# Modulation rows, one sum product, a context norm and the final norm moved to other places in a two-layer backbone kernel

## The chip, the cores and the metric

The kernel runs on one core of a Trainium2 chip. The metric is the device time of one execution in microseconds (us). The engines are named PE (TensorE: PE for matmuls, PEld for weight loads), DVE (VectorE), ACT (ScalarE), POOL (GpSimd) and SP (SyncE, which issues most of the loads). Line numbers, as in L1263, are lines of the kernel before.

## What is computed

Two layers over 512 latent tokens `x` and 256 context tokens `ctx`, width 1024, all in float32. Each layer has an attention part and a SwiGLU feed-forward part (FFN, hidden width 2816). Ahead of each stands an RMSNorm with shift and scale, behind each a gated residual; shift, scale and gate come from a product of the conditioning vector with `ada_w`. In layer 1 the context is used for keys and values only. At the end stands an RMSNorm of the latent tokens.

```python
for layer in range(2):
    ctx_out = layer < 1
    mod_x = split((silu(c) @ ada_w[layer] + ada_b[layer]), 6)        # s = 0 .. 5; s = 5 is the FFN's gate
    mod_c = split(silu(c_ctx) @ ada_w[layer] + ada_b[layer], 6)
    h_x = rmsnorm(x, norm_g[layer, 0]) * (1 + mod_x[1]) + mod_x[0]   # h_c the same from ctx and mod_c
    o_x, o_c = mixer(h_x, h_c)                # layer 0: differential heads || 2-D neighbourhood heads
                                              # layer 1: windowed grouped-query attention with sinks
    x = x + mod_x[2] * o_x
    h_x = rmsnorm(x, norm_g[layer, 1]) * (1 + mod_x[4]) + mod_x[3]
    x = x + mod_x[5] * ((silu(h_x @ w1) * (h_x @ w3)) @ w2)
    if ctx_out:                               # the same three lines for ctx with mod_c
        ...
return rmsnorm(x, final_g)
```

## The kernel before

**Number format.** Activations lie transposed, features on partitions in eight tiles of 128. A float32 product is three matmuls: every operand is split into a high part (made on ACT) and a low part (the rest, made on DVE), and `mm3` adds high x high, low x high and high x low in one PSUM bank. `split` makes both parts with ACT and DVE; `split_by_dma` has the low part made by an accumulating DMA issued on POOL.

**Stages.** Layer 0's attention goes by eight pairs of heads (`u` = 0 to 7; from 4 on they are neighbourhood heads). A list of steps (four blocks of latent queries and one of the context, each with a first part `a`: scores and softmax, and a second part `b`: transposes and value product) is interleaved with fillers: the next pair's projections, modulation rows, and in the last pair the first half of the output projection (`prep`, `first_part`). Then come the FFN of layer 0, the attention of layer 1, and the FFN of layer 1.

**Weights.** A class `Stream` holds a list of weights in the order of use (`S.add`, `S.add_made`). `S.next()` hands out the next one, makes the parts of some items ahead and requests the loads of some more. Raw weights lie in three buffers (`raw` of `wpool`), parts in three (`wh`, `wl`). All weight loads are on SP's queue, in order.

**The order on an engine.** The program is written as one sequence, and a scheduler places its instructions on each engine by a simulated timeline, within the dependencies; so an engine's order can differ from the order of the text. `tc.issue_after(x)` keeps an instruction behind `x`. A tile taken from a pool waits until the readers of what lay in its buffer are done.

**Modulation rows.** For s = 2 to 4 of layer 0, and for s = 5 of layer 0 and all of layer 1, the product with `ada_w` is done on DVE: a row loads 512 KB (`raw`) and multiplies it with the two conditioning vectors, with the sums into `mod` (`ada_rows`, L269, L270). The first 24 rows (`row_pieces`) are fillers of pairs 4 to 6. The other 56 (`ada1`, the eight of s = 5 first) are done in layer 0's FFN by `rows(n, after)`, which keeps them behind a given instruction and requests the next load (`ada_request`, two buffers).

**FFN of layer 0.** Hidden tiles go by pairs `p` = 0 to 10. Pairs 0 and 1 are plain products (`plain_tile`). The others use a scheme of seven half-size products in place of eight (`seven`, for `w1` and for `w3`): it takes sums of weights (`pair_weights0`, L496 to L500) and of tokens. `token_sums` makes the token sums `t2`, `t3`, `t4`; `first_sum`, run after pair 1, makes `t1` in place of a part of `hb`. Their order in `seven` is (`b11`, `b21`), `t1`, (`t2`, `b22`), (`t3`, `t4`); the results are added up by L1263 to L1271, which also free the PSUM banks (`f`, eight of one buffer each). The down products (`down`) of a group run between the `w1` and the `w3` products of the next group's first pair; `to_residual` (L1275) adds them to `xr` and `cr` with the gate of s = 5.

**The end of that FFN.** `down_last` does the last group: first all token products, then the context products `m` = 0 to 7. After the context product `m` = 2 stands `next_norm`, the norm of the tokens for layer 1 (sums of squares in `sq_sum`; `rstd_of`, whose matmul with ones is L309; `h_make`, L350 to L352). After the last context product stands the context's norm, in slices of a `q` tile. `behind_g` splits the weights `w_c[8]` and `w_c[10]` behind the making of `g`; `w_c[11]` is split by the ordinary path (L158, L159). Layer 1's attention begins with `k_x(0)`, then `v_part` for the groups 1 and 2 (latent tokens) and 0 (context), then `k_c(0)`.

**The tail.** `down_last` of layer 1 goes by halves of the tokens. After its second half's third product stands `final_norm(0)`: squares and sums, the scaling by `final_g` on ACT (L1720), `rstd_of`, the products with the reciprocal root on DVE and POOL and the output DMAs (L1723, L1724). After the last product stands `final_norm(1)`. The norm's tiles share few buffers:

```python
        npool = PoolMap(
            ns_a0=(fp, "s", 2), ns_a1=(fp, "s", 2), ns_s=(fp, "q", 2), ns_h=(fp, "q", 2),
            ns_v=(fp, "s", 2), ns_y=(fp, "s", 2), ns_t=(fp, "s4", 1),
        )
```

Of the kernel before, what the change touches and what calls it, by code (L numbers as in the profile page):

```python
# [16 lines left out]
D = 1024  # L17
# [20 lines left out]
def tile_trunk(  # L38
# [265 lines left out]

    def rstd_of(ps, accs, dim, pool):
# [39 lines left out]
    def h_make(k, h, xk, r, l, i, v, pool):  # L345
# [6 lines left out]
        nc.vector.scalar_tensor_tensor(h[:, 1, :], t, b, f32(h[:, 0, :]), op0=ALU.add, op1=ALU.subtract)  # L352
# [132 lines left out]

    def pair_weights0(p):

        raws = []

        def fn(n, raw):  # L490
            add = nc.vector.tensor_add
            if n == 0:
                raws[:] = raw
# [15 lines left out]
        def add_w(w):  # L509
            for i in range(4):  # L510
# [18 lines left out]
    def behind_g(raw):  # L529
        hi, lo = S.part_tiles()  # L530
        with tc.issue_after(g_made[0].ins):
            nc.scalar.copy(hi, raw[0])
        with tc.issue_after(g_made[1].ins):
            nc.vector.tensor_sub(lo, raw[0], f32(hi))
# [5 lines left out]
    def weights0():  # L540
# [23 lines left out]
        for j in (8, 10):  # L564
            S.add_made([w_c[j]], behind_g)
        for j in (11, 9, 0, 1, 2, 3, 4, 5, 6, 7):
# [4 lines left out]


    ada1 = [(l, s_, k) for l, s_ in [(0, 5)] + [(1, z) for z in range(6)] for k in range(KT)]
    ada1_load, ada_raw = list(range(len(ada1))), []

    def ada_request(pool):
        if ada1_load:
            raw = pool.tile([P, 1024], F32, tag="ada", name="raw")
            nc.sync.dma_start(raw, ada_wT[ada1_load.pop(0)])
# [3 lines left out]
    with ExitStack() as st:  # L583
# [394 lines left out]
        rows = [(s_, k) for s_ in range(2, 5) for k in range(KT)]  # L978

        def row_pieces(n):  # L980
# [8 lines left out]
            for _ in range(n):  # L989
                s_, k = rows.pop(0)  # L990
                S.add(ada_wT0[s_ - 2, k], "ada")
# [23 lines left out]
        for u in range(8):  # L1015
# [14 lines left out]
            else:  # L1030
                for m in range(KT):
                    S.add(wo_ab[m])

# [45 lines left out]
                fl = [prep(0), prep(1), prep(2), prep(3)] + [first_part(t) for t in range(4)] + [prep(4), prep(5), prep(6)]  # L1079
# [37 lines left out]
    with ExitStack() as st:  # L1117
# [123 lines left out]
        def seven(c, u, first=lambda: None):  # L1241
# [19 lines left out]
            (g1,) = item("t1")  # L1261
# [3 lines left out]
            add(u, g2, u)  # L1265
            add(c[1], g1, u)
# [34 lines left out]
        def down_last(js):  # L1301
# [10 lines left out]
            for m in range(KT):  # L1312
# [547 lines left out]
```

## Time and profile before

| | before |
|---|---|
| median of 3 runs | 1652.71 us (1646.57 to 1653.13) |
| profiled execution, its own time | 1649.52 us |
| its span, first to last instruction | 1647.7 us |
| mean granted TensorE clock | 0.989 |
| busy: PE / PEld / DVE / ACT / POOL | 1567.5 / 1402.1 / 1251.1 / 749.2 / 272.6 us |
| rows L269 | 80 x 1.22 us |
| read from HBM | 160.45 MB |

A line of the timeline gives start, duration, engine, line, operation, output <- input with sizes and count, and in brackets the idle time of the engine just before it with what ended it. Ends of matmuls are modelled, and consecutive ones overlap. A "q" behind an engine's name stands for its queue of issued DMAs. In a line of stretches the busy times of PE, PEld, DVE, ACT and POOL are followed by the granted clock, the DMA engines' share and GB/s.

### The profile page before, as it was taken

To read this page: it belongs to the slowest core of one execution; us is meant where nothing else is said; L and a number is where in the kernel's file an instruction comes from. 1 tells how busy PE (TensorE), PEld (TensorE's weight loads), DVE (VectorE), ACT (ScalarE), POOL (GpSimd) and SP (SyncE) were. 2 spreads that over 40 slices of the span, in tenths; PEclk is the share of its full clock that TensorE was granted. 3 is DMA by queue.
4 is the path that set the end of the run, shared out by engine and by line. 5 is a ranking of instruction groups with operands and counts; after the bars stand their busy time and mean duration, and the time that the engine had idled before them with its cause. 6 is when DMAs were issued, how large, how long until landed. Compare 5 with 4: busy or idle time off the path is not lost.

```text
span 1647.7 us, 26339 instructions
## 1 busy us (share of the span) xinstructions
PE 1567.5 (95%) x10222; PEld 1402.1 (85%) x10222; DVE 1251.1 (76%) x2155; ACT 749.2 (45%) x1326; POOL 272.6 (17%) x313
## 2 busy tenths in 40 slices
PE   5999998999999899999999998999999999999996
PEld 3798887877888789999999996977788799989896
DVE  4758698976576888879798879587665987869685
ACT  4446554556244423333434254356655552525243
POOL 2222222345010000010100001254322000000001
PEclk9999999999999999999999999999999999999998
DMA  9323254644225556675766762411010432323321
GB/s 340 100 58 89 80 157 131 189 133 119 69 64 131 155 163 160 159 199 159 193 182 170 201 173 94 101 54 40 14 39 25 156 128 78 127 74 95 120 73 52
DMA packets 69508, 199.52 MB, mean 121 GB/s; under 512 B 6932, under 2 KB 19380, under 8 KB 69384
## 3 DMA queue, kind: packets, MB, share of 16 engines
q1 hardware_dynamic: 59464, 164.40, 32.1%
q0 software_dynamic: 9344, 32.92, 9.4%
q8 instruction: 81, 1.33, 0.3%
q10 hardware_dynamic: 576, 0.52, 0.1%
q14 instruction: 43, 0.35, 0.1%
HBM read 160.45 MB, written 4.86 MB: 100 GB/s over the span
## 4 chain that ended last, share of the span: by engine, by line
PE 58%; issue 7%; DMA 6%; DVE 6%; ACT 2%; POOL 0%; DVEq 0%; SPq 0%; POOLq 0%; ACTq 0%
PE f L1250 4%; PE f L1251 4%; PE f L1249 4%; PE f L1653 4%; PE f L1652 4%; PE f L1651 4%; PE f L1281 3%; PE f L1282 3%; PE f L1283 3%; DMA wl<-raw 2%; PE lin L207 2%; PE t L1485 2%; PE lin L208 2%; PE lin L209 2%; PE f L1705 2%
## 5 line engine op out<-in xcount | busy, mean ns | idle before, releaser
L196 ACT ACTIVATE wh<-raw 128x1024 fp32r<-128x1024 f32 (+1 forms) x94 | 90.2, 976 | 233.9 <-DVE raw L500 124.4
L207 PE MATMUL lin<-hb,wh 128*128 128x512 f32 (+1 forms) x456 | 161.3, 354 | 8.5 <-DVE q L369 2.2
L208 PE MATMUL lin<-hb,wh 128*128 128x512 f32 (+1 forms) x456 | 159.4, 349 | 0.1
L209 PE MATMUL lin<-hb,wl 128*128 128x512 f32 (+1 forms) x456 | 158.3, 347 | 0.0
L197 DVE TENSOR_TENSOR wl<-raw,wh 128x1024 fp32r<-128x1024 f32 (+1 forms) x94 | 104.7, 1119 | 34.7 <-ACT wh L196 32.6
L269 DVE SCALAR_TENSOR_TENSOR junk<-raw,tables 128x1024 bf16<-128x1024 f32 x80 | 97.6, 1220 | 20.1 <-DMA raw<-in_ada_wT_dram 19.8
L202 POOL DMA_DIRECT2D wl<-raw x41 | 35.7, 871 | 458.6 <-ACT wl L201 421.6
L1281 PE MATMUL f<-g,wh 128*128 128x512 f32 (+1 forms) x304 | 103.4, 342 | 6.0 <-DVE q L1263 5.0
L207 PEld LDWEIGHTS lin<-hb,wh 128*128 128x128 f32 x456 | 86.1, 189 | 22.8 <-issue 3.0
L159 DVE TENSOR_TENSOR wl<-raw,wh 128x1024 fp32r<-128x1024 f32 x62 | 81.4, 1313 | 29.8 <-ACT wh L158 27.0
L1282 PE MATMUL f<-g,wh 128*128 128x512 f32 (+1 forms) x304 | 103.4, 341 | 0.0
L1283 PE MATMUL f<-g,wl 128*128 128x256 f32 (+1 forms) x304 | 101.9, 338 | 1.2 <-DMA wl<-raw 1.2
L1652 PE MATMUL f<-hb,wh 128*128 128x256 f32 x360 | 101.7, 283 | 0.0
L1651 PE MATMUL f<-hb,wh 128*128 128x256 f32 x360 | 101.4, 283 | 0.0
L1653 PE MATMUL f<-hb,wl 128*128 128x256 f32 x360 | 101.2, 283 | 0.0
L158 ACT CAST wh<-raw 128x1024 fp32r<-128x1024 f32 x62 | 64.9, 1047 | 77.5 <-PE lin L208 23.6
L1250 PE MATMUL f<-hb,wh 128*128 128x384 f32 x288 | 96.3, 335 | 1.1 <-DVE hb L197 1.1
L1249 PE MATMUL f<-hb,wh 128*128 128x384 f32 x288 | 96.4, 335 | 0.7 <-ACT hb L196 0.7
L1251 PE MATMUL f<-hb,wl 128*128 128x384 f32 x288 | 96.3, 334 | 0.3 <-DMA wl<-raw 0.3
L208 PEld LDWEIGHTS lin<-hb,wh 128*128 128x128 f32 x456 | 86.3, 189 | 11.0 <-issue 0.9
L209 PEld LDWEIGHTS lin<-hb,wl 128*128 128x128 f32 x456 | 86.2, 189 | 10.3 <-issue 0.3
L336 POOL TENSOR_TENSOR ns_a<-ns_a,ns_s 128x256 f32<-128x256 f32 (+1 forms) x16 | 17.3, 1084 | 442.7 <-ACT ns_s L332 434.4
(397 smaller groups left out, 4953.7 us busy)
## 6 DMA issues: line engine op xcount, KB each, us to landing
raw<-in_w_dram SPq DMA_DIRECT2D x132, 512.0 KB, 3.8
raw<-in_ada_wT_dram SPq DMA_DIRECT2D x80, 512.0 KB, 4.2
wl<-raw POOLq DMA_DIRECT2D x41, 512.0 KB, 6.4
raw<-in_w_ab_dram SPq DMA_DIRECT2D x24, 512.0 KB, 4.4
raw<-in_ada_w_dram SPq DMA_DIRECT2D x16, 512.0 KB, 9.5
k<-k SPq DMA_DIRECT2D x16, 384.0 KB, 6.0
raw<-in_w_c_dram SPq DMA_DIRECT2D x12, 512.0 KB, 4.3
nb<-in_na_bias_dram POOLq DMA_DIRECT2D x16, 256.0 KB, 3.8
```

The source lines that it names most:

```text
L207: nc.tensor.matmul(ps, wh(k), xh(k), start=k == 0, stop=False)
L208: nc.tensor.matmul(ps, wh(k), xl(k), start=False, stop=False)
L209: end = nc.tensor.matmul(ps, wl(k), xh(k), start=False, stop=k == n - 1)
L1249: nc.tensor.matmul(ps, wh(k), b[:, 0, :], start=k == 0, stop=False)
L1250: nc.tensor.matmul(ps, wh(k), b[:, 1, :], start=False, stop=False)
L1251: nc.tensor.matmul(ps, wl(k), b[:, 0, :], start=False, stop=k == 3)
L1281: nc.tensor.matmul(ps, hi, g[:, 0, cols[v]], start=first, stop=False)
L1282: nc.tensor.matmul(ps, hi, g[:, 1, cols[v]], start=False, stop=False)
L1283: nc.tensor.matmul(ps, lo, g[:, 0, cols[v]], start=False, stop=last)
L1651: nc.tensor.matmul(ps, wh(k), b[:, 0, :], start=k == 0, stop=False)
L1652: nc.tensor.matmul(ps, wh(k), b[:, 1, :], start=False, stop=False)
L1653: nc.tensor.matmul(ps, wl(k), b[:, 0, :], start=False, stop=k == 3)
```

## The change

- The eight rows of layer 0's FFN gate (s = 5) become fillers of the last pair of heads: four ahead of the output weights in the stream, four between the first of these, in kind `ada` (their raw buffers are those of the weights). The FFN's own rows are 48, all of layer 1; none runs in pair 1 or after pair 2's `w1` products, two instead of one stand behind each piece of the first down product.
- For pair 2's `w1` the product with `t1` comes last (`late_sum`), its weight part is made last, and the results are added in another order.
- `next_norm` stands after the context product `m` = 4 instead of 2. The context's sums of squares stay at the end of the FFN; its reciprocal root and `h_make` go behind `k_x(0)` in layer 1's attention, into that stage's buffers.
- `w_c[11]` is split behind the fourth tile of the token norm (`h_made[3 - KT]`, the fifth from the end of the list).
- The second half's final norm gets accumulators and root in the buffers of `spool[0]`. The first half's output products and DMAs (`put_out(0)`) stand behind the last residual add.

```diff
 h_make:
-        nc.vector.scalar_tensor_tensor(h[:, 1, :], t, b, f32(h[:, 0, :]), op0=ALU.add, op1=ALU.subtract)
+        h_made.append((act, nc.vector.scalar_tensor_tensor(h[:, 1, :], t, b, f32(h[:, 0, :]), op0=ALU.add, op1=ALU.subtract)))
...
+    def late_sum(p, w):
+        return p == supers0[1][0] and w is w1
 pair_weights0:
-            if n == 1:
+            if n and not done:
                 add(spool0[0], a21, a22)
                 add(a21, a21, a11)
+                done.append(n)
...
-            for i in range(4):
+            for i in (0, 2, 3, 1) if late_sum(p, w) else range(4):
...
+        S.add_made([w_c[11]], lambda raw: behind(*h_made[3 - KT], raw[0]))
-        for j in (11, 9, 0, 1, 2, 3, 4, 5, 6, 7):
+        for j in (9, 0, 1, 2, 3, 4, 5, 6, 7):
             S.add(w_c[j])
...
-    ada1 = [(l, s_, k) for l, s_ in [(0, 5)] + [(1, z) for z in range(6)] for k in range(KT)]
+    ada1 = [(1, z, k) for z in range(6) for k in range(KT)]
...
-        rows = [(s_, k) for s_ in range(2, 5) for k in range(KT)]
+        rows = [(s_, k) for s_ in range(2, 6) for k in range(KT)]
...
+                rr = row_pieces(4)
                 for m in range(KT):
                     S.add(wo_ab[m])
+                    if m < 4:
+                        rr += row_pieces(1)
...
-                fl = [prep(0), prep(1), prep(2), prep(3)] + [first_part(t) for t in range(4)] + [prep(4), prep(5), prep(6)]
+                fl = [prep(m) for m in range(4)] + [first_part(t) for t in range(4)]
+                fl = [f for pair in zip(fl, rr) for f in pair] + [prep(4), prep(5), prep(6)]
...
 seven:
             p1, p2 = item("b11", "b21")
             nc.scalar.copy(u, p1)
-            (g1,) = item("t1")
+            if not late:
+                (g1,) = item("t1")
             g2, r3 = item("t2", "b22")
             add(c[0], p2, u)
             first()
             add(u, g2, u)
+            if late:
+                g3, r4 = item("t3", "t4")
+                nc.vector.scalar_tensor_tensor(c[3], g3, -1.0, u, op0=ALU.mult, op1=ALU.subtract)
+                add(c[2], r4, c[3])
+                (g1,) = item("t1")
+                add(c[1], g1, u)
+                nc.vector.tensor_sub(c[3], c[3], g1)
+                return add(c[1], r3, c[1])
...
 down_last of layer 0:
-                if m == 2:
+                if m == 4:
                     next_norm()
             q = q_tile()
-            pool = Carve([q[:, NC * i : NC * i + NC] for i in range(6)])
-            r = rstd_of(fps(), sq_sum(cr, pool), D, pool)
-            for k in range(KT):
-                h_make(k, hc[k], cr[k], r, 1, 0, 1, pool)
+            sums = [spool0[0][:, NC * i : NC * i + NC] for i in range(2)]
+            c_sums.extend(sq_sum(cr, Carve(sums + [q[:, NC * i : NC * i + NC] for i in range(2)])))
...
-                        end = plain_tile(2 * p + i, g)
-                        if p:
-                            rows(3, end)
-                        elif i:
+                        plain_tile(2 * p + i, g)
+                        if i and not p:
                             token_sums()
...
-                    rows(2 if p == 2 else 1, end)
+                    rows(1 if p > 2 else 0, end)
                     if late:
-                        down(hidden(supers0[n - 1]), (2,) if n > 2 else (1,))
+                        down(hidden(supers0[n - 1]), (1,) if n == 2 else (2,))
...
 attention of layer 1:
         k_x(0, w0)
+        r = rstd_of(linp(), c_sums, D, npool)
+        for k in range(KT):
+            h_make(k, hc[k], cr[k], r, 1, 0, 1, npool)
...
 FFN of layer 1:
+        def norm_tiles(i):
+            a = (spool[0], "sum", 2) if i else (fp, "s", 2)
+            return PoolMap(ns_a0=a, ns_a1=a, ns_s=(fp, "q", 2), ns_v=(fp, "s", 2), ns_y=a, ns_t=(fp, "s4", 1))
...
-            r = rstd_of(fps(), sq, D, npool)
+            gains.append((ts, rstd_of(fps(), sq, D, pool)))
+
+        def put_out(i):
+            ts, r = gains[i]
             for k in range(KT):
                 (nc.gpsimd if k in (1, 4, 7) else nc.vector).tensor_mul(ts[k], ts[k], r)
-                (nc.scalar if i and k % 2 else nc.sync).dma_start(out[:, k, c], ts[k])
+                (nc.scalar if i and k % 2 else nc.sync).dma_start(out[:, k, halves[i]], ts[k])
...
+            with tc.issue_after(end.ins):
+                put_out(0)
             final_norm(1)
+            put_out(1)
```

More of the change, by code (lines that the diff above doesn't have):

```diff
@@ L484, in tile_trunk @@
     supers0 = [[0, 1], [2], [3, 4], [5, 6], [7, 8], [9, 10]]
+    def late_sum(p, w):
+        return p == supers0[1][0] and w is w1
     def pair_weights0(p):
-        raws = []
+        raws, done = [], []
         def fn(n, raw):
@@ L492, in fn @@
             if n == 0:
-                raws[:] = raw
+                raws[:], done[:] = raw, []
             (a11, a12), (a21, a22) = ([half(z, i) for i in range(2)] for z in raws)
-            if n == 1:
+            if n and not done:
                 add(spool0[0], a21, a22)
                 add(a21, a21, a11)
+                done.append(n)
             if n == 2:
@@ L527, in tile_trunk, with behind @@
     g_made = []
-    def behind_g(raw):
+    def behind(act, dve, raw):
         hi, lo = S.part_tiles()
[L531 to L534, printed above, removed]
+        with tc.issue_after(act.ins):
+            nc.scalar.copy(hi, raw)
+        with tc.issue_after(dve.ins):
+            nc.vector.tensor_sub(lo, raw, f32(hi))
         return hi, lo
@@ L564, in weights0 @@
         for j in (8, 10):
-            S.add_made([w_c[j]], behind_g)
-        for j in (11, 9, 0, 1, 2, 3, 4, 5, 6, 7):
+            S.add_made([w_c[j]], lambda raw: behind(*g_made, raw[0]))
+        S.add_made([w_c[11]], lambda raw: behind(*h_made[3 - KT], raw[0]))
+        for j in (9, 0, 1, 2, 3, 4, 5, 6, 7):
             S.add(w_c[j])
     spool0, tpool, small_parts = [], [], []
-    ada1 = [(l, s_, k) for l, s_ in [(0, 5)] + [(1, z) for z in range(6)] for k in range(KT)]
+    c_sums = []
+    ada1 = [(1, z, k) for z in range(6) for k in range(KT)]
     ada1_load, ada_raw = list(range(len(ada1))), []
@@ L578, in ada_request @@
             raw = pool.tile([P, 1024], F32, tag="ada", name="raw")
-            nc.sync.dma_start(raw, ada_wT[ada1_load.pop(0)])
+            nc.sync.dma_start(raw, ada_wT[KT + ada1_load.pop(0)])
             ada_raw.append(raw)
@@ L990, in row_pieces @@
                 s_, k = rows.pop(0)
-                S.add(ada_wT0[s_ - 2, k], "ada")
+                S.add(ada_wT0[s_ - 2, k] if s_ < 5 else ada_wT[k], "ada")
                 out_.append(lambda s_=s_, k=k: f(s_, k))
@@ L1239, in plain_tile, with seven @@
             return split(gt[j][:, 0, :], gt[j][:, 1, :], z)
-        def seven(c, u, first=lambda: None):
+        def seven(c, u, first=lambda: None, late=False):
             def product(name, part):
@@ L1341, in tile_trunk @@
                     c = [q[:, H * i : H * i + H] for i in range(4)]
-                    end = seven(c, s_tile())
+                    end = seven(c, s_tile(), late=late_sum(p, w1))
                     act = nc.scalar.activation(q, q, AF.Silu)
@@ L1692, in to_residual @@
         def to_residual(m, ps, c):
-            nc.vector.scalar_tensor_tensor(x1[m][:, c], ps, mod[1][:, 5, 0, m : m + 1], x1[m][:, c], op0=ALU.mult, op1=ALU.add)
+            return nc.vector.scalar_tensor_tensor(x1[m][:, c], ps, mod[1][:, 5, 0, m : m + 1], x1[m][:, c], op0=ALU.mult, op1=ALU.add)
         def down(js):
@@ L1708, in down @@
                     to_residual(4 * i + m, ps[m], slice(0, NX))
-        fo = []
+        fo, gains = [], []
+        def norm_tiles(i):
+            a = (spool[0], "sum", 2) if i else (fp, "s", 2)
+            return PoolMap(ns_a0=a, ns_a1=a, ns_s=(fp, "q", 2), ns_v=(fp, "s", 2), ns_y=a, ns_t=(fp, "s4", 1))
         def final_norm(i):
             c = halves[i]
-            sq = sq_sum([x1[k][:, c] for k in range(KT)], npool, apart=i == 1)
+            pool = norm_tiles(i)
+            sq = sq_sum([x1[k][:, c] for k in range(KT)], pool, apart=i == 1)
             ts = []
@@ L1735, in down_last @@
                     )
-                    to_residual(m, ps, c)
+                    end = to_residual(m, ps, c)
                     if ci and m == 2:
                         final_norm(0)
+            with tc.issue_after(end.ins):
+                put_out(0)
             final_norm(1)
+            put_out(1)
         for n, sg in enumerate(supers):
```

1 line of the change is left out of this document (added).

## The prediction

> **What bounds the kernel now.** I read the first part of the page, then the waits of TensorE, then busy time by stretches, and only then the timeline around each wait.
>
> ```profile
> PE 1567.5 (95%) x10222; PEld 1402.1 (85%) x10222; DVE 1251.1 (76%) x2155; ACT 749.2 (45%) x1326; POOL 272.6 (17%) x313
> ```
>
> TensorE is busy for 1567.5 of 1647.7 us, and the change leaves its matmuls as they are in number and size. So the change can win only out of 80 us of TensorE idling, plus what TensorE loses at a lower clock. The waits say where that idling lies (waiter, releaser: total, times, longest):
>
> ```profile
> PE t L235 <- DMA raw<-in_ada_w_dram: 13.5, 3, 12.7
> PE f L309 <- DVE q L338: 5.5, 1, 5.5
> PE f L1281 <- DVE q L1263: 5.0, 1, 5.0
> PE f L309 <- DVE ns_a L338: 3.6, 1, 3.6
> PE f L309 <- DVE norm L338: 2.6, 1, 2.6
> ...
> PE f L1250 <- DVE hb L197: 1.1, 1, 1.1
> ...
> PE f L1249 <- ACT hb L196: 0.7, 1, 0.7
> ```
>
> The longest, the first weights' load, is not touched. The others are: two norms at the end of the first FFN (5.5, 2.6), its first down product (5.0), the first seven products' wait for the token sum `t1` (0.7 + 1.1), the final norm (3.6). The change reaches every one. What it adds goes where VectorE still has room (stretch, length; PE, PEld, DVE, ACT, POOL busy; clock; DMA):
>
> ```profile
> 285.00:335.00 50.00, 49.69 (x353) 43.74 (x352) 45.17 (x84) 23.57 (x54) 18.97 (x22) 1.00 0.57 181
> ...
> 340.00:385.00 45.00, 41.55 (x323) 32.72 (x322) 25.95 (x58) 25.90 (x70) 24.64 (x38) 1.00 0.47 134
> 385.00:440.00 55.00, 51.77 (x357) 42.39 (x355) 36.94 (x60) 27.24 (x57) 13.25 (x22) 1.00 0.32 96
> 553.00:580.00 27.00, 19.78 (x106) 17.95 (x105) 22.89 (x42) 10.92 (x17) 2.59 (x3) 0.92 0.77 215
> 580.00:612.00 32.00, 32.00 (x180) 28.21 (x179) 26.59 (x47) 7.83 (x8) 1.74 (x2) 0.96 0.53 140
> ```
>
> **1. The gate's eight rows leave the start of the FFN, and `t1` comes last.** One row is a 512 KB load and two VectorE products with their accumulator reads:
>
> ```profile
> L269 DVE SCALAR_TENSOR_TENSOR junk<-raw,tables 128x1024 bf16<-128x1024 f32 x80 | 97.6, 1220 | 20.1 <-DMA raw<-in_ada_wT_dram 19.8
> ...
> 572.10 0.08 DVE L270 DVE_READ_ACCUMULATOR junk<-raw,csr 128x1 f32 x1
> 572.10 1.02 DVE L197 TENSOR_TENSOR hb<-q,hb 128x384 fp32r<-128x384 f32 x2
> 577.07 1.22 DVE L269 SCALAR_TENSOR_TENSOR junk<-raw,tables 128x1024 bf16<-128x1024 f32 x1 [3.94 <-DMA raw<-in_ada_wT_dram]
> 578.22 0.55 DVE L1263 TENSOR_TENSOR q<-f,s 128x384 f32<-128x384 f32 x1
> ...
> 592.00 0.17 DVE L272 TENSOR_TENSOR mod<-mod,adab 128x16 f32<-128x16 f32 x1
> 592.21 4.29 DVE L1275 SCALAR_TENSOR_TENSOR res<-f,mod,res 128x512 f32<-128x512 f32 x8
> ```
>
> So a row costs VectorE 2 x 1.22 + 2 x 0.08 = 2.6 us, eight 20.8. Read the timeline as a chain: VectorE works through rows and `first_sum` until 573.1, then stands at the fifth row for 3.94 us because its load has not landed; behind it in order stands the add L1263, which frees a PSUM bank; TensorE waits for that bank. The residual adds (L1275) cannot run before 592.2, since the gate they multiply by is finished at 592.0 (L272). After the change no row runs between the plain pair and the first down product, the gate is there long before, and `t1`, made by `first_sum`, is wanted only behind `t2`, `b22`, `t3`, `t4`. The waits 5.0, 1.1 and 0.7 go: 6.8 us. The stall also cost clock:
>
> ```profile
> 578.83:590.21 11.38, 11.38 (x48) 9.50 (x49) 11.24 (x20) 3.25 (x4) 0.32 (x1) 0.85 0.30 102
> ...
> 1022.77:1031.53 8.76, 8.76 (x35) 7.21 (x35) 8.54 (x16) 4.78 (x9) 0.00 (x0) 0.81 0.08 32
> ```
>
> Behind it the granted clock is 0.85 over 11.38 us, 0.15 x 11.38 = 1.7 us. [...]
>
> What may be late next: the first down product now takes two rows a piece, so 580 to 612 holds about two rows more, 26.59 + 5.2 = 31.8 of 32 us on VectorE. It is full, but TensorE has the banks of one piece in hand; I charge 0.5. The changed order of weight parts (0, 2, 3, 1) makes both sums of weights ahead of the second item; these are the same adds, their input is free only once the accumulating DMA has read it, before as after, so nothing. Term: 6.8 + 1.7 - 0.5 = **+8.0** (ends: 3, if another bank wait takes over half of the 5.0 and its clock; 8.5).
>
> **2. What the rows cost in the last head pair.** 20.8 us of VectorE, eight 512 KB loads on SP's queue, in turn with the output weights in the same three raw buffers, and past the loads of earlier heads' outputs (`ar`) on that queue. Rows ran in the stretch from 285 on: there VectorE is 90% busy and TensorE idles 0.3 us. From 340 to 440 VectorE has 62.9 of 100 us, with the rows 83.7, still under those 90%. So most is hidden by matmuls. It is not free: TensorE already idles 3.4 + 3.2 us there, on chains through VectorE, ScalarE and GpSimd, and a row in front of a mask-and-maximum step delays it by up to 1.22 us. Ends: 0 (no work is taken away here, a gain is excluded) and 20.8 (no cover). Nearest is the 285 stretch; I take **-2.5**, about one and a half rows. If the cover fails, the weights are late next: a row holds the buffer in which the next of them lands. GpSimd is in these chains too, and rows slow it:
>
> ```profile
> 303.58 2.69 POOL L914 TENSOR_SCALAR p<-p,rs 128x512 f32<-128x512 f32 x2
> ...
> 322.63 3.69 POOL L950 TENSOR_SCALAR pc<-pc,rs 128x256 f32<-128x256 f32 x4 [8.46 <-DVE rs L766]
> ...
> 360.42 1.83 POOL L950 TENSOR_SCALAR pc<-pc,rs 128x256 f32<-128x256 f32 x4 [4.99 <-DVE rs L766]
> ...
> 377.32 1.35 POOL L914 TENSOR_SCALAR p<-p,rs 128x512 f32<-128x512 f32 x2
> ```
>
> The same scalings take 2.69 and 3.69 us in the stretch with rows, 1.35 and 1.83 in the one without. The last pair has four of the one and one of the other: 4 x 1.34 + 1.86 = 7.2 us at most, a rival below. [...]
>
> **3. End of the first FFN.**
>
> ```profile
> 996.10 0.75 DVE L1275 SCALAR_TENSOR_TENSOR res<-f,mod,res 128x512 f32<-128x512 f32 x1
> ...
> 1007.25 2.84 PE L309 MATMUL f<-norm,ones 128*128 128x512 f32 x6 [2.63 <-DVE norm L338]
> ...
> 1014.34 1.41 DVE L350 SCALAR_TENSOR_TENSOR norm<-res,amod,csr 128x512 f32<-128x512 f32 x2
> ...
> 1017.72 1.22 DVE L159 TENSOR_TENSOR wl<-raw,wh 128x1024 fp32r<-128x1024 f32 x1
> ...
> 1022.77 2.08 PE L309 MATMUL f<-q,ones 128*128 128x256 f32 x4 [5.50 <-DVE q L338]
> ...
> 1029.06 0.75 DVE L352 SCALAR_TENSOR_TENSOR hb<-norm,mod,hb 128x512 fp32r<-128x512 f32 x1
> ```
>
> With eight rows fewer in all, three left over ahead of the residual adds go (7.8 us of VectorE), and the adds no longer trail. The token norm's sum of squares is then ready early, and its matmul, two context products later in the order, finds no wait. But it still starts near 1007: what was waiting becomes context work. Then everything hangs on VectorE: first L350 7.1 us after that matmul, eight tiles made at 2 x 0.67 = 1.34 us each. Before, the last tile was done at 1029.7. After, the context's rescaling no longer stands between (three ops of 0.4 us), nor part of its sums and residual adds; the weight split L159 stays, only behind the fourth tile. I expect the last tile at about 1028, one more step of k's product, and the context's L309, now behind it, 1 us: 1.5 us sooner than the row 1022.77:1031.53 lets it be. So the waits 2.6 and 5.5 go but are mostly given back as short waits at VectorE's pace. The 24 context `h_make` instructions move into the attention stage, hidden by the two token v groups ahead of the first user. Term: **+1.5** (ends: -1 if that cover is short; 5.5 + 1.7 = 7.2 if the tiles keep pace).
>
> **4. The tail.**
>
> ```profile
> 1628.96 2.84 DVE L1723 TENSOR_TENSOR fo<-fo,ns_y 128x256 f32<-128x256 f32 x5
> ...
> 1631.72 0.47 DVE L1693 SCALAR_TENSOR_TENSOR res<-f,mod,res 128x256 f32<-128x256 f32 x1
> ...
> 1631.89 0.42 ACT L329 ACTIVATE ns_a<-res 128x256 f32<-128x256 f32 x1 [2.40 <-DVE fo L1723]
> ...
> 1634.28 2.08 PE L309 MATMUL f<-ns_a,ones 128*128 128x256 f32 x4 [3.55 <-DVE ns_a L338]
> ...
> 1636.15 1.06 PE L309 MATMUL f<-ns_s,ones 128*128 128x256 f32 x2
> ...
> 1637.25 0.47 ACT L313 ACTIVATE ns_t<-f,epst 128x256 f32<-128x256 f32 x1 [2.88 <-PE f L309]
> ...
> 1639.65 3.34 DVE L1723 TENSOR_TENSOR fo<-fo,ns_y 128x256 f32<-128x256 f32 x5
> ```
>
> Half 0's five output products stand ahead of half 1's residual adds, and half 1's accumulators wait for the buffer which those products read. With other buffers and the products behind the last add, squares run as residuals come. TensorE ends at 1634.28 - 3.55 = 1630.7; add 0.47, square 0.42, last matmul about 0.5: 1632.3 against 1637.2, 4.9 less. Half 0's products (2.84 us) and eight output DMAs on SP now run in the shadow of half 1's logarithm, exponential and square; VectorE may hold one step back for a product or two: 0.7. Term: **+4.2** (ends 1.5, if all of the 2.84 stands ahead of half 1's steps, and 4.9).
>
> **Sum.** 8.0 - 2.5 + 1.5 + 4.2 = 11.2 us. The profiled execution took 1649.5 (span 1647.7 and 1.8 around it), so 1638.3; the median 1652.7 is 3.2 above it, so 1641.5. I take **1641**.
>
> **Rivals.**
> - *GpSimd's stretch lies on the path.* 7.2 in place of 2.5: 1646. For it the four rows of GpSimd above; against it GpSimd's 24.64 of 45 us.
> - *The bank wait moves.* Part 1 gives 3: 1646. For it the 31.8 of 32 us on VectorE; against it TensorE's unbroken 32.00 of 32 in that stretch before.
> - *Half 0's outputs still stand ahead.* Part 4 gives 1.5: 1644.
> - *Slower: VectorE becomes the bound of the last head pair.* If rows interleave one to one with the steps and each stands ahead of what TensorE waits for, the parts give 13.7 - 20.8 = -7.1: 1660, and more if weights come late behind their buffers. It decides from 13.7 us exposed, two rows in three. Against it the 285 stretch.
>
> **How the numbers follow.** Forecast 0.50, GpSimd 0.17, bank wait 0.14, outputs 0.10, slower 0.09. About 0.5% (8 us) is what a measurement of this kernel tells from no change: under 1644 it is faster. That takes most of the forecast and some of the next three, 0.58; slower by over 0.5% needs more than full exposure of the rows, 0.07; the rest 0.35. Range 1632 (nothing charged for the rows, upper ends at the FFN's end) to 1652 (two of the middle rivals together).
>
> **What would show it.** Right: no wait of L1281 on L1263 and clock 1.00 at the FFN's start; the wait on `q` L338 gone, with several short waits on `hb` in its place; last L313 some 5 us nearer to the end of the down product; TensorE's idling from 340 to 440 up by 2 to 3 us. Wrong: that idling up by over 10 us, or a new wait over 3 us for a weight, a bank or the context's tiles.

## The result, and the profile after

The kernel after takes 1641.75 us in the median of 5 runs (1639.9 to 1643.57); the ratio to the kernel before is 0.9942, 95% interval 0.9927 to 0.9958. The forecast was 1641. The time came out as forecast, but largely by luck: two of the four terms are far off, step 2 (five times its price) and step 3 (four times its gain), and these two misses nearly cancel. Line numbers from here on are those of the kernel after, except in the experiments that start from the kernel before.

The first part of the page shows what the prediction read first: TensorE's matmuls are as before, 1571 us busy of a span of 1640.3.

```profile
span 1640.3 us, 26342 instructions
...
PE 1571.1 (96%) x10222; PEld 1405.2 (86%) x10222; DVE 1253.5 (76%) x2155; ACT 748.8 (46%) x1326; POOL 275.5 (17%) x313
```

TensorE's waits after (waiter, releaser: total, times, longest):

```profile
PE t L235 <- DMA raw<-in_ada_w_dram: 13.5, 3, 13.1
PE f L1305 <- DVE q L1290: 3.9, 1, 3.9
PE s L911 <- DMA k<-k: 3.8, 2, 2.0
PE t L981 <- DVE pt L974: 3.2, 2, 2.6
PE t L934 <- ACT at L948: 3.0, 2, 2.5
...
PE t L945 <- DVE pt L937: 2.0, 2, 1.8
```

The six waits of before that the prediction listed behind the first load are gone from the head of the list (the final norm's is 0.7 us now). In their place stand one new wait for a PSUM bank (L1305) and four kinds of wait in the first attention that have grown (L911 to L981; of L911's 3.8 us only the 2.0 are new, the rest lies ahead of pair 5 and was there before, with 1.7).

To place the difference I cut both profiled executions at the same events: the mask-and-maximum that opens head pair 5 (the ninth L914); the first matmul with ones of the FFN's latent norm (L312); the first matmul of pair 2's `w3` products; the first context product of the first FFN's `down_last`; the first matmul of `k_x(1)`; the last matmul of the last down product; the end of the last matmul with ones. The stretches between them, in us:

| stretch | before | after | difference | predicted |
|---|---|---|---|---|
| start to pair 5 (same code) | 317.31 | 315.13 | -2.18 | 0 |
| A: pairs 5 to 7, output projection | 156.04 | 167.75 | **+11.71** | +2.5 |
| B: FFN start, to pair 2's `w3` | 136.56 | 126.68 | **-9.88** | -8.0 |
| C: to `down_last`'s context part | 390.24 | 393.33 | +3.09 | 0 |
| D: end of the FFN, to `k_x(1)` | 50.81 | 44.33 | **-6.48** | -1.5 |
| E: second layer | 579.49 | 579.95 | +0.46 | 0 |
| F: tail, to the last norm matmul | 6.76 | 2.57 | **-4.19** | -4.2 |

They add up to -7.47, the spans differ by 7.4; the medians differ by 10.96 and the ratio makes it 9.6 us (7 to 12), so the profiled pair lies at the low end. A stretch also differs between executions of the same code: C is 388.5 to 392.3 us in the four kernels below that have before's code there (before, e1, e2, e10), and the start to pair 5 is 315.1 to 318.8 in all.

The stretches of the prediction's windows, in the order it had them (length; PE, PEld, DVE, ACT, POOL busy; clock; DMA):

```profile
340.00:385.00 45.00, 36.94 (x253) 28.37 (x253) 40.90 (x78) 21.80 (x54) 26.61 (x32) 0.92 0.66 196
385.00:440.00 55.00, 50.57 (x354) 40.28 (x353) 33.55 (x61) 30.67 (x70) 15.70 (x27) 0.97 0.37 105
553.00:580.00 27.00, 27.00 (x158) 25.52 (x157) 23.23 (x43) 14.90 (x22) 2.59 (x3) 1.00 0.50 112
580.00:612.00 32.00, 32.00 (x185) 28.36 (x185) 25.40 (x44) 8.31 (x9) 1.74 (x2) 1.00 0.63 168
```

The FFN's start is what was forecast: no idling, clock 1.00. The attention is not. From 340 to 440 TensorE idles 8.06 + 4.43 = 12.5 us, against 3.45 + 3.23 = 6.7 before, and the clock, 1.00 before, is 0.92 and 0.97: 0.08 x 45 + 0.03 x 55 = 5.3 us more. Idling 5.8 and clock 5.3 make 11.1 of the 11.7 us of stretch A.

### The profile page after: what moved, and what is told of

Same layout as the page of the kernel before. It is cut to its first block, busy times and chain, and to the rows that moved or that the text cites. A ratio compares the mean times of both kernels' runs of the same rounds, so it can differ in the third digit from the quotient of the medians.

```text
span 1640.3 us, 26342 instructions
## 1 busy us (share of the span) xinstructions
PE 1571.1 (96%) x10222; PEld 1405.2 (86%) x10222; DVE 1253.5 (76%) x2155; ACT 748.8 (46%) x1326; POOL 275.5 (17%) x313
## 4 chain that ended last, share of the span: by engine, by line
PE 79%; DVE 10%; DMA 5%; issue 3%; ACT 1%; POOL 0%; SPq 0%; DVEq 0%; ACTq 0%; POOLq 0%
PE f L1264 5%; PE f L1266 5%; PE f L1265 5%; PE f L1676 4%; PE f L1675 4%; PE f L1674 4%; PE lin L207 3%; PE lin L208 3%; PE f L1305 3%; PE f L1306 3%; PE f L1307 3%; PE lin L209 3%; PE f L207 3%; PE f L208 3%; PE f L209 3%
## 5 line engine op out<-in xcount | busy, mean ns | idle before, releaser
L269 DVE SCALAR_TENSOR_TENSOR junk<-raw,tables 128x1024 bf16<-128x1024 f32 x80 | 99.3, 1241 | 13.7 <-DMA raw<-in_ada_wT_dram 13.2
L1305 PE MATMUL f<-g,wh 128*128 128x256 f32 (+1 forms) x304 | 103.8, 343 | 3.9 <-DVE q L1290 3.9
L1306 PE MATMUL f<-g,wh 128*128 128x256 f32 (+1 forms) x304 | 103.4, 341 | 0.0
```

The lines of the kernel that those rows point to most:

```text
L1305: nc.tensor.matmul(ps, hi, g[:, 0, cols[v]], start=first, stop=False)
L1306: nc.tensor.matmul(ps, hi, g[:, 1, cols[v]], start=False, stop=False)
```

## The experiments

Each kernel was timed in five rounds against the kernel before; the table gives the ratio and the stretches of its profiled execution.

| kernel | median us | ratio (95% interval) | A | B | C | D | F |
|---|---|---|---|---|---|---|---|
| before | 1652.71 | 1 | 156.0 | 136.6 | 390.2 | 50.8 | 6.8 |
| after | 1641.75 | 0.9942 (0.9927 to 0.9958) | 167.8 | 126.7 | 393.3 | 44.3 | 2.6 |
| e1 tail only | 1647.18 | 0.9971 (0.9958 to 0.9984) | 156.1 | 138.0 | 392.0 | 51.1 | 2.6 |
| e2 FFN end only | 1643.53 | 0.9952 (0.9935 to 0.9970) | 155.7 | 136.9 | 388.5 | 45.0 | 6.8 |
| e3 gate rows out | 1630.02 | 0.9864 (0.9844 to 0.9884) | 154.9 | 126.7 | 391.2 | 43.8 | 2.6 |
| e4 rows late | 1637.20 | 0.9918 (0.9898 to 0.9937) | 162.4 | 126.7 | 391.1 | 44.4 | 2.6 |
| e5 rows and `t1` only | 1648.42 | 0.9978 (0.9960 to 0.9996) | 170.5 | 126.7 | 391.0 | 47.9 | 6.8 |
| e6 `t1` in order | 1642.41 | 0.9942 (0.9920 to 0.9965) | 166.2 | 126.7 | 394.6 | 43.8 | 2.6 |
| e7 rows held in pair 7 | 1642.43 | 0.9943 (0.9922 to 0.9964) | 166.7 | 126.7 | 394.2 | 44.4 | 2.6 |
| e8 rows spread | 1635.71 | 0.9908 (0.9886 to 0.9929) | 160.1 | 126.7 | 393.9 | 44.1 | 2.6 |
| e9 `v` held | 1649.33 | 0.9993 (0.9980 to 1.0006) | 165.5 | 126.7 | 393.8 | 49.4 | 2.6 |
| e10 FFN end, norm at `m` = 2 | 1647.27 | 0.9973 (0.9958 to 0.9989) | 156.0 | 137.6 | 392.3 | 47.6 | 6.0 |
| e11 spread, sums on GpSimd | 1633.99 | 0.9897 (0.9881 to 0.9913) | 160.7 | 126.7 | 391.5 | 44.3 | 2.6 |
| e12 rows short | 1638.47 | 0.9926 (0.9908 to 0.9944) | 164.1 | 126.7 | 392.9 | 44.1 | 2.6 |

Two theories went in. T1, from the table of stretches: the rows cost about 11 us in the attention, the FFN's start pays 10, its end 6.5, the tail 4. T2, the prediction's terms: 2.5, 8.0, 1.5, 4.2.

**e1: the tail alone.** The kernel before with the new final norm:

```diff
+        def norm_tiles(i):
+            a = (spool[0], "sum", 2) if i else (fp, "s", 2)
...
+            with tc.issue_after(end.ins):
+                put_out(0)
             final_norm(1)
+            put_out(1)
```

> The kernel before with the final norm's part alone (norm_tiles, put_out, the returned residual update). Both theories sum the whole 11 us gain from parts, and this part at 4.1 to 4.2 us: about 4 us under the kernel before (0.9975 of its time; 1648.5 if it stands at 1652.7), nothing moved ahead of 1627 us, the last L309 matmul of the norm some 7 us nearer the end of the down product. Rival: the final norm is worth less alone, because half 0's multiplications and outputs were hidden anyway: 1.5 us.

Measured: 0.9971, 4.8 us, and stretch F goes from 6.76 to 2.57, in this kernel as in after. The tail is a part by itself, worth what was forecast.

**e2: the end of the FFN alone.** The kernel before with `next_norm` after `m` = 4, the context's sums kept, the rest of its norm behind `k_x(0)` and `w_c[11]` split behind a tile of the token norm:

```diff
-                if m == 2:
+                if m == 4:
                     next_norm()
...
         k_x(0, w0)
+        r = rstd_of(linp(), c_sums, D, npool)
+        for k in range(KT):
+            h_make(k, hc[k], cr[k], r, 1, 0, 1, npool)
```

> The kernel before with the end of the first FFN alone changed (x norm after the fifth context product, context's sums at the end of the FFN, the rest of its norm behind k_x(0), w_c[11] behind a context tile). Theory T1, from the milestones of the two traces: the start of k_x(1) comes 6.5 us nearer the start of the last down product, so 6.5 us under the kernel before (0.996). Theory T2, the prediction's step: 1.5 us under it (0.999), the waits given back at VectorE's pace; the 6.5 us of the trace would then hang on something that the other parts do.

Measured: 0.9952, and stretch D falls by 5.8, without any other part. That is T1; the step's 1.5 is wrong.

**e10: the same, with the norm again after `m` = 2.**

```diff
-                if m == 4:
+                if m == 2:
```

> The kernel before with the new end of the first FFN, but the x norm started after the third context product as in before, not after the fifth. It parts the 6.4 us of the kernel with the whole new end. Theory T1: the move to the fifth product is worth the 2.63 us wait on the x norm's sums that the third has, so about 4 us under before (0.9975), with a wait of about 2.6 us on L311 that comes back near 1007 us. Rival: the norm started earlier ends earlier, its h tiles are ready when the down product ends, and this kernel is as fast as the whole new end or faster (0.995 or less), since the 1.5 us wait on hb at the start of k_x(0) goes.

Measured: 0.9973, stretch D 47.6, and the wait of 2.88 us on the norm's sums stands there again, at 1010 us. So D's gain of 5.8 is 3.3 for the context norm behind `k_x(0)` (with the split of `w_c[11]`) and 2.5 for the two products.

**e9: the `v` products held behind `k_x(0)`.** On after:

```diff
-            v_group(ps, g, w)
+            with tc.issue_after(k_end.ins):
+                v_group(ps, g, w)
...
-        k_x(0, w0)
+        k_end = k_x(0, w0)
```

> The kernel after with the v products (L399 to L401) held until the first k product over the x tokens (k_x(0)) has ended, so that they can't stand between its matmuls. Theory T1: these products are what PE does while VectorE makes the eight h tiles (1018.6 to 1030.7 us in after, 12.1 us, of which k_x(0) alone fills 6). Without them PE idles 5 to 6 us more between 1018 and 1031, in short waits on hb, as the prediction had it, and the time is 5 to 7 us over after (1646.5 to 1648.5). Theory T2 (the v products fill nothing that matters, the gain is the removed wait on q and the context's norm behind k_x(0) alone): as after, within 1.5 us.

Measured: 0.9993, 7.6 us over after, a little beyond T1's range; in the profile stretch D is 49.4, 5.1 more than after and 1.4 less than before (the profiled execution is the fastest of this kernel, 1646.64 us, so the stretches don't hold the whole 7.6). The 1.4 is close to the prediction's +1.5. The timeline of this kernel shows the short waits that it described:

```profile
1017.83 0.50 PE L208 MATMUL t<-hb,wh 128*128 128x512 f32 x1 [0.46 <-DVE hb L355]
...
1025.06 0.50 PE L208 MATMUL t<-hb,wh 128*128 128x512 f32 x1 [1.66 <-DVE hb L355]
...
1026.72 0.50 PE L208 MATMUL t<-hb,wh 128*128 128x512 f32 x1 [0.70 <-DVE hb L355]
...
1028.38 0.50 PE L208 MATMUL t<-hb,wh 128*128 128x512 f32 x1 [0.70 <-DVE hb L355]
```

In after, at the same place, the `v` products (L399 to L401) stand between the `k` matmuls and need the same tiles:

```profile
1018.62 0.50 PE L207 MATMUL t<-hb,wh 128*128 128x512 f32 x1 [1.49 <-ACT hb L354]
1018.95 0.40 PE L399 MATMUL t<-wh,hb 128*128 128x256 f32 x2
1019.58 0.80 PE L208 MATMUL t<-hb,wh 128*128 128x512 f32 x1 [0.23 <-DVE hb L355]
1020.18 0.63 PE L209 MATMUL t<-hb,wl 128*128 128x512 f32 x1
1020.60 0.63 PE L207 MATMUL t<-hb,wh 128*128 128x512 f32 x1
1021.03 0.41 PE L400 MATMUL t<-wh,hb 128*128 128x256 f32 x1
...
1023.57 0.81 PE L312 MATMUL lin<-res,ones 128*128 128x256 f32 x3
```

Each tile that VectorE finishes feeds both the three matmuls of `k_x(0)` and those of the two latent `v` groups, so TensorE keeps step (busy for 11.00 of 11 us from 1020 to 1031), and the context's L312 comes without a wait.

**e5: the rows and `t1` alone.** After with the old end of the FFN and the old tail (`next_norm` at 2, the context's norm at the end, the final norm as before).

> The kernel before with the moved gate rows and the last t1 alone (old end of the first FFN, old final norm). Theory T1 (attention loses 9 to 11.5 us to the rows, the FFN start gains 10, the down product of pair 3 gives back 1 to 3): no gain that can be told, 0.998 to 1.001 of the kernel before. Theory T2, the prediction's steps 1 and 2 (gain 8.0, cost 2.5): 5.5 us faster, 0.9967.

Measured: 0.9978. The interval holds the prediction's 0.9967 and about half of T1's range, so the time doesn't tell them apart. The stretches do: A is 14.5 us longer than before, B 9.8 shorter. D is 2.9 shorter with the old code there: fewer rows are left ahead of the residual adds, and the wait of 2.63 us goes by that alone, as the prediction said.

**e6: `t1` third again.** On after:

```diff
     def late_sum(p, w):
-        return p == supers0[1][0] and w is w1
+        return False
```

> The kernel after with t1 again third in the first seven products of pair 2 (the rows stay where after has them). If t1's place carries a part of the gain at the FFN start, one of the waits of before returns there (0.48 to 1.09 us each, 565 to 574 us in before, or 4.97 us at the first down product), and this kernel is 1 to 5 us slower than after (1643 to 1647 beside 1641.75). If the rows alone filled VectorE there, it stands within 1 us of after and the waits stay away.

Measured: 0.9942, as after; B is 126.68 in both, and TensorE has no wait from 553 to 612 us. Once the rows are out of the FFN's start, the place of `t1` is worth nothing that shows.

**e3: the eight rows left out.** On after, neither loaded nor multiplied (the gate is zero):

```diff
+    nc.gpsimd.memset(mod[0][:, 5], 0.0)
...
-                ada_rows(0, s_, k, [tables, rbuf], S.next(), junk)
+                if s_ < 5:
+                    ada_rows(0, s_, k, [tables, rbuf], S.next(), junk)
...
-                S.add(ada_wT0[s_ - 2, k] if s_ < 5 else ada_wT[k], "ada")
+                if s_ < 5:
+                    S.add(ada_wT0[s_ - 2, k], "ada")
```

> The kernel after with the eight gate rows left out of the last head pair altogether (neither loaded nor multiplied; the FFN's gate is set to zero, so the output lacks the first FFN's contribution); everything else as in after. Theory T1: the eight rows cost the attention 9.5 to 11.5 us, since they run in the steps of pair 6 in which VectorE has no idle time: 9.5 to 11.5 us under the kernel after (1630 to 1632 beside 1641.75). Theory T2, the prediction's step: they cost 2.5 us: 1639. Were the loss in attention from another thing in the change (the order of the weight loads around pair 7, a run's difference), this kernel would stand where after stands.

Measured: 0.9864, 0.78% or 12.9 us under after, and A is 154.9 (12.8 us under after). The rows, loads included, are the price, and it is five times the term.

**e7: the rows kept in pair 7.** In after the scheduler had put them earlier than the text has them: row instructions of the gate start at 337.05, beside the steps of pair 6. Here each is held until its own step:

```diff
+                        step_mx[0] = nc.vector.tensor_tensor_reduce(
...
+                if s_ == 5:
+                    with tc.issue_after(step_mx[0].ins):
+                        ada_rows(0, s_, k, [tables, rbuf], raw, junk)
```

> The kernel after with each gate row held until the attention step of the last head pair in which the program text puts it (behind that step's row maximum), so that the eight rows run in pair 7 and not in pair 6, where after ran them. This is the place that the prediction priced at 2.5 us. If that price was right and only the place was wrong: 7 to 9 us under after (1633 to 1635), no new waits at 340 to 380 us. If VectorE bounds the last head pair (the prediction's slower rival): as after or slower, with the 13 us of idling moved to 380 to 435 us. Between: 1636 to 1640, the rows cost about 5 us there.

Measured: 0.9943, as after; A is 166.7. The rows are where the prediction had them, and cost as much. Its stretches show the price moved from the first to the second, with VectorE 95% busy:

```profile
340.00:385.00 45.00, 41.06 (x303) 32.12 (x301) 21.91 (x50) 22.95 (x64) 23.55 (x39) 0.97 0.35 96
385.00:440.00 55.00, 45.95 (x316) 35.76 (x315) 52.30 (x89) 29.78 (x60) 18.80 (x20) 0.99 0.52 174
```

So the size was wrong, not the place: this is the prediction's slower rival in part. In the five kernels with the rows in the last two pairs stretch A is 9.5 to 14.5 us longer than before, not 20.8.

**e12: the rows loaded, but multiplied over 8 of 1024 columns** (the gate is wrong by that):

```diff
+                n = D if s_ < 5 else 8
+                ada_rows(0, s_, k, [z[:, 0:n] for z in (tables, rbuf)], S.next()[:, 0:n], junk[:, 0:n])
```

> The kernel after with the eight gate rows loaded as in after (8 x 512 KB on SP's queue) and multiplied over their first 8 of 1024 columns alone, so that each of the 16 row instructions takes VectorE a tenth of its time (the FFN's gate is wrong by that). It parts the rows' loads from their 22 us on VectorE; the kernel without the rows left both out and was 11 us under after. Theory V: VectorE's time is the whole price, so this kernel stands where that one did, within 2 us (0.9864 to 0.988 of before). Theory L: the loads pay a part, since they stand on SP's queue ahead of the transfer of k halves and of weights (the wait on k<-k was 2.02 us in after and 0.91 in before): 3 us or more of the 11 remain (0.989 or more).

Measured: 0.9926, only 0.16% (2.6 us) under after, with overlapping intervals; A is 164.1, 3.6 under after and 9.2 over e3. That is Theory L: VectorE's time is not the whole price. With most of it gone (0.17 us a product in place of 1.22), VectorE reaches the rows before their loads have landed and stands there:

```profile
DVE pt L937 <- PE t L934: 6.9, 3, 2.8
DVE junk L269 <- DMA raw<-in_ada_wT_dram: 6.5, 4, 2.1
```

and ScalarE waits 4.2 us once for an output weight whose load stands behind the rows' on SP's queue; the DMA engines are 69% busy from 340 to 385 us (66% in after, 48% in e3). In after no row waits for its load from 320 to 440 us. One wait of TensorE can be followed back to the loads: the copy L974 stands behind two rows that wait, and TensorE behind the copy.

```profile
341.17 0.17 DVE L269 SCALAR_TENSOR_TENSOR junk<-raw,tables 128x8 bf16<-128x8 f32 x1 [2.14 <-DMA raw<-in_ada_wT_dram]
...
343.03 0.17 DVE L269 SCALAR_TENSOR_TENSOR junk<-raw,tables 128x8 bf16<-128x8 f32 x1 [1.48 <-DMA raw<-in_ada_wT_dram]
...
343.13 0.69 DVE L974 COPY pt<-t 128x512 f32<-128x512 f32 x1
...
343.87 1.08 PE L981 MATMUL t<-pt,v 128*64 128x256 f32 x6 [2.05 <-DVE pt L974]
```

So the loads and the rows' places in VectorE's order, with little of VectorE's time, are enough for 9.2 of the 12.8 us of stretch A. Whether VectorE's time alone would cost as much isn't shown: no kernel had the rows' time without their loads, none had the loads without the rows, and none had the loads at another place in the queue alone.

**e4: the rows one behind each product of the output projection's second half.** On after:

```diff
-                rr = row_pieces(4)
+                rr = []
                 for m in range(KT):
                     S.add(wo_ab[m])
-                    if m < 4:
-                        rr += row_pieces(1)
+                    if m > 3:
+                        rr += row_pieces(2)
...
-            w = S.next(0 if t >= 2 else 2)
+            w = S.next(2)
...
                 wo_chunk(m, w, "x", 4)
+                rr.pop(0)()
```

So the loads of the rows move with them, and the parts of two items are made ahead in all of that half.

> The kernel after with the eight gate rows taken out of the last head pair and put one behind each product of the second half of the output projection (430 to 475 us, PE without idle time, VectorE about half busy). Theory T1: the 9.5 to 11.5 us come back but for a little: 1631 to 1634, faster than both kernels. Theory T2: 1639 to 1641. Rival: the 8 x 3.3 us on VectorE there hold up the residual updates and so the projection's banks and the FFN norm: then a new wait on L1076 or L1083 or a later norm matmul, and no gain.

Measured: 0.9918; A is 162.4, 5.3 under after, about half of what T1 hoped. Two rows still ran at 371 and 377 us, beside the steps of attention. TensorE now waits for residual updates that stand behind rows, 4.3 us in five waits from 400 to 480:

```profile
PE lin L207 <- DVE res L1076: 3.2, 3, 1.6
PE lin L207 <- DVE res L1083: 1.1, 2, 0.6
```

A product of that half takes TensorE 12 x 0.23 = 2.8 us, a row and an update 2.6 + 0.75 = 3.35 on VectorE: a single product doesn't cover a row.

**e8: half as dense.** Four rows behind every second product, four behind the held context products, each held until the context product before it:

```diff
                     if m > 3:
                         rr += row_pieces(1)
+                rr += row_pieces(4)
...
-            w = S.next(0 if t >= 2 else 2)
+            w = S.next(2)
...
+                    with tc.issue_after(before[0].ins):
+                        ada_rows(0, s_, k, [tables, rbuf], raw, junk)
...
+                if m % 2:
+                    rr.pop(0)()
```

> The kernel after with four of the eight gate rows behind every second product of the second half of the output projection and four behind its held context products, each held until the context product before it. The run with one row behind each product won 4 us and paid 4.4 us of bank waits (L1076 and L1083) and 1.8 us for two rows that ran at 370 to 383 us. Theory T1: with half as many rows a product the bank waits fall under 1.5 us and the two early rows are gone: 1632 to 1634, 8 to 10 us under after. If the residual updates wait for the rows all the same: 1637, as the run with one a product.

Measured: 0.9908, 1635.71; A is 160.1, 7.7 under after. The time lies just above the expected 1632 to 1634. One row still ran early, at 368 us, in spite of the hold, and the waits for residual updates (L1082, L1089) are 2.0 us in place of 4.3. The wait for a PSUM bank in the FFN is 4.1 us here (L1315 on L1300), as in after.

**e11: e8 with two sums of weights on GpSimd.**

```diff
-                add(spool0[0], a21, a22)
-                add(a21, a21, a11)
+                eng = nc.gpsimd if p == supers0[2][0] and first_w[0] else nc.vector
+                first_w[0] = False
+                eng.tensor_add(spool0[0], a21, a22)
+                eng.tensor_add(a21, a21, a11)
```

> The kernel with the gate rows spread over the output projection, and in it the two sums of weight blocks of pair 3's first seven products (L502 and L503 in after, 128x512) on GpSimd in place of VectorE. In after VectorE waited 7.04 us in L502 for a weight's load, with the addition that frees PSUM (L1290) behind it, and PE waited 3.94 us for that; the spread kernel had 4.13 us there. Theory: it is the order on VectorE; with the sum elsewhere the wait falls under 1.5 us and the kernel is 2 to 4 us under the spread one (1632 to 1634). Rival: the load itself is late, and PE waits the same time a product later for the weight t1: 1635 to 1637.

First the wait that it aims at, in after's timeline:

```profile
637.21 0.55 DVE L1281 TENSOR_TENSOR s<-f,s 128x384 f32<-128x384 f32 x1
644.81 0.69 DVE L502 TENSOR_TENSOR res<-raw 128x512 f32<-128x512 f32 x1 [7.04 <-DMA raw<-in_w_dram]
645.42 0.55 DVE L1290 TENSOR_TENSOR q<-f,s 128x384 f32<-128x384 f32 x1
...
646.02 0.58 PE L1305 MATMUL f<-g,wh 128*128 128x256 f32 x1 [3.94 <-DVE q L1290]
```

VectorE stands 7 us at the sum L502 for a weight's load, and behind it in order stand the additions that free the banks. Measured: 0.9897, 1633.99. My edit missed: it moved the sums of pair 3's `w1`, which run at 607 us, and the blocking one belongs to its `w3`. The order on VectorE changed all the same, as this kernel shows:

```profile
632.62 0.56 DVE L1304 SCALAR_TENSOR_TENSOR q<-f,q 128x384 f32<-128x384 f32 x1
...
640.70 0.69 DVE L504 TENSOR_TENSOR res<-raw 128x512 f32<-128x512 f32 x1 [5.00 <-DMA raw<-in_w_dram]
...
643.95 0.64 PE L1317 MATMUL f<-g,wh 128*128 128x512 f32 x1 [2.32 <-DVE res L1311]
```

Now all additions stand ahead of the sum, the sum still waits, and TensorE loses 2.3 us in place of 4.1, for a residual add. Stretch C is 2.3 shorter than e8's. So the place of that sum among the additions matters; that GpSimd helped is not shown. By time e11 and e8 can't be told apart; e11 and after can (0.9913 against 0.9927 where their intervals are nearest). By median it is the fastest version that computes everything.

## Why the prediction was right, point by point

- **The total** was right largely by luck. Against the forecast stand +9.2 us (step 2) and +3.1 (stretch C), and on the other side -1.9 (step 1's own stretch), -5.0 (step 3), and 2.2 by which the profiled run was ahead at 315 us. With 0.5 in the second layer that leaves 3.7 us in this profiled pair: 7.5 were gained, not 11.2. By the ratio it is 9.6, by the medians 10.96; the median of before from which the forecast was counted, 1652.7, lies 1.3 to 1.9 above the four that were taken with the experiments (1650.8 to 1651.4).
- **Step 1** (predicted 8.0): stretch B gave 9.9, somewhat more than the 6.8 of waits and 1.7 of clock. Its charge of 0.5 for what is late next was too small, and its place a little off: from 580 to 612 VectorE was busy for 25.40 of 32 us, not 31.8, and TensorE had no wait there (32.00 of 32 us), but a bank wait of 3.94 us came one down product later, at 642, and for the same reason as the old one: a VectorE instruction waits for a load, and an addition that frees a bank stands behind it. That is the rival "the bank wait moves". What it costs is not sharp: C is 3.1 us longer than in this profile of before, 1 to 5 longer than in the four profiles of before's code, which have shorter waits there of their own (0.5 to 2.5 us). With the 3.1, the net of step 1 is 6.8. The `t1` part of the edit did nothing that shows (e6).
- **Step 2** (predicted -2.5) is the step that failed, by a factor of five: 11.7 in the profile, 12.9 by time against e3. Its sentence "still under those 90%. So most is hidden by matmuls" took VectorE's fullness for the measure of cover. After has VectorE 40.9 of 45 us busy, 91%, just as in the stretch taken as nearest, and TensorE idles 8 us there and not 0.3. What differs is TensorE's own work, and the kernel before shows it, in the groups of TensorE's instructions from 285 to 335 us:

```profile
L207 PE MATMUL lin<-hb,wh 128*128 128x512 f32 (+1 forms) x38 | 13.3, 351 | 0.0
...
L397 PE MATMUL lin<-wh,hb 128*128 128x256 f32 x37 | 10.8, 291 | 0.0
...
L934 PE MATMUL t<-pt,v 128*64 128x128 f32 x50 | 5.0, 283 | 0.3 <-DVE pt L926 0.3
```

  and from 340 to 385:

```profile
L934 PE MATMUL t<-pt,v 128*64 128x128 f32 x112 | 10.2, 282 | 0.8 <-DVE pt L926 0.6 <-ACT pt L928 0.2
L923 PE MATMUL t<-ident,p 128*128 128x128 f32 x58 | 9.1, 283 | 1.2 <-ACT at L937 1.2
L209 PE MATMUL lin<-hb,wl 128*128 128x256 f32 (+1 forms) x21 | 7.1, 336 | 0.0
```

  In the first, 223 matmuls of projections (112 of `mm3`, 111 of `v_group`) wait for nothing that VectorE is busy with; in the second there are 62, and most of the rest are transposes and value products at the end of a chain through VectorE and ScalarE. There rows in front of copies became waits of TensorE: in after the row product at 369.31 (1.54 us) stands just ahead of the copy L937 and that at 376.24 (1.20 us) ahead of the copy L974, and TensorE waits 1.82 and 2.64 us for these two. The step also charged no clock: 5.3 us of the price in this execution of after, and 1.7 to 6.8 over stretch A in the five kernels with the rows in the last two pairs. And it listed the loads and costed them at nothing, while e12, which has the loads and almost none of VectorE's time, keeps 9.2 of the 12.8 us. So both terms were mis-sized; how the price divides between VectorE's time and the loads stays open.
- **The rivals on step 2.** VectorE as the bound came true in part: 9.5 to 14.5 of the 20.8 us are exposed, about the 13.7 from which it would have decided. GpSimd's scalings did get longer in after, by 4.2 us in three places (3.15, 3.05 and 2.57 us beside 1.36, 1.83 and 1.35 in before); no wait of TensorE from 330 to 440 us ends on GpSimd, and whether they lie on a longer chain was not measured. The runs show that they were longer, not why.
- **Step 3** (predicted +1.5): 6.5 in the profile, 5.8 alone (e2). "Mostly given back as short waits at VectorE's pace" is what happens when TensorE has `k_x(0)` only (e9: 1.4 left of the gain). The text named the `v` groups as cover for the context's tiles; it overlooked that the scheduler may also put them between the matmuls of `k_x(0)`. That was its upper end, 7.2, "if the tiles keep pace".
- **Step 4** (predicted +4.2): 4.19 in stretch F. Its sum was off by 0.2: 1630.7 + 0.47 + 0.42 + 0.5 is 1632.1, not 1632.3, and the term by it 4.4. The rows that carry it, in after:

```profile
1627.17 0.28 PE L209 MATMUL f<-g,wl 128*128 128x256 f32 x1
1628.13 1.13 PE L312 MATMUL f<-ns_a,ones 128*128 128x256 f32 x4 [0.69 <-DVE ns_a L341]
1629.10 0.64 PE L312 MATMUL f<-ns_s,ones 128*128 128x256 f32 x2
```

  The last matmul with ones ends at 1629.74, 2.6 us behind the last product; before it was 6.8.
- **Its own signs.** Of the signs for "right" the FFN's start, the wait on `q` and the tail came true. The several waits on `hb` did not, to the kernel's good. Idling from 340 to 440 rose by 5.8, between the "2 to 3" and the "over 10"; with the clock it is 11. The new wait over 3 us for a bank is there.

## What to carry to other kernels

An engine's free time is not cover: ask what the engine that sets the pace has to do meanwhile that waits for none of this, and count those instructions in the very stretch. The same eight rows with their loads cost 12.8 us among transposes and copies and 5.2 mostly among projections (stretch A of after and of e8 against e3's; one of e8's rows still ran early). Count the loads too: they were enough for most of the price. And one late load became a wait of what stood behind it in order: in after VectorE stood 7.04 us at the sum L502, the addition L1290 came behind it, and TensorE waited 3.94 us. So look at what is next in the queue behind every instruction that waits for a load.

## What was not expected of the hardware

In after, TensorE's granted clock fell behind shorter waits than the two behind which the prediction's rows show it low (5.0 and 5.5 us; 0.85 and 0.81). The longest wait at the end of the FFN is 1.49 us, and the granted clock of the next stretch is 0.50:

```profile
1018.00:1020.00 2.00, 1.15 (x4) 0.91 (x5) 2.00 (x4) 1.54 (x3) 0.58 (x2) 0.90 0.59 169
1020.00:1022.00 2.00, 2.00 (x8) 1.71 (x8) 2.00 (x5) 0.84 (x2) 0.00 (x0) 0.50 0.32 126
...
1024.00:1026.00 2.00, 2.00 (x13) 1.81 (x12) 2.00 (x3) 1.48 (x5) 0.00 (x0) 1.00 0.00 0
```

In the attention, behind the wait of 2.47 us that ends at 350.38, the clock is 0.75 from 352 to 356.

But the same wait didn't always bring it. The wait of 1.49 us at the end of the FFN is there in e3, e4, e6, e7, e8, e9, e11 and e12 too: the half clock followed in e4, e7, e9 and e11, where 128x512 matmuls behind it take 0.63 us (as in after), and not in e3, e6, e8 and e12, where most of them take 0.39 to 0.40 us. Nor did it follow four waits of 0.49 to 1.66 us in 6 us (e9, 1024 to 1030: most take 0.39 to 0.40 us). So in these runs neither the length of a wait nor the share of idling decided alone; what did was not settled. A gain or a loss of clock read from one profile is for that reason uncertain; an estimate is 1.7 us for each such wait, half of the 3.4 us for which the granted clock was 0.50 in after (350.6 to 354.0 and 1019.6 to 1023.0).
